# Wider matmuls for the head-norm sums and the spatial bias in a hybrid decoder kernel

## The chip, the cores and the metric

The program runs on all 8 NeuronCores of one Trainium2 chip. Each core works on one prompt sequence of 2048 tokens and on 16 of the 128 sample sequences (8 tokens each); the cores exchange nothing. The metric is the device time of the slowest core, in microseconds (us).

Some executions fall in a second, slower state, in which the cores of a die (cores 0 to 3 or 4 to 7) are granted a lower TensorE clock. Ratios below use fast runs only; a median is over all runs of a kernel, slow ones too, so a median of a kernel with several slow runs says little. Even in fast runs a pair of cores can be a little slow (clock 0.97 in place of 0.98), and the slowest of eight is a noisy number. For effects of a few us I therefore also use the **core mean**: the mean span of the cores of a run, averaged over the runs of a kernel, without cores whose granted clock is more than 0.007 below the median clock of that kernel. The "±" beside a core mean is twice the standard error over executions.

## The reference, cut to what matters

Two layers; each mixes three branches and then runs a feed-forward block. The change touches two places:

```python
# branch A: the output of the gated linear attention, per head of 256 channels
o = rms_norm(o, gla_norm) * jax.nn.silu(g_out)
# branch C: spatial gating within chunks of 128 positions, 4 head groups
w = w_s * tril
mixed = jnp.einsum('gts,ncsgd->nctgd', w, vg) + b_s.T[None, None, :, :, None]
return u * mixed
```

## The kernel before: the parts that matter

All matmuls but the transposes go through one helper. It waits for the operands, issues a list of matmuls and lets the last one signal. In the tuples the fourth and fifth entries are `start` and `stop` of an accumulation. All of these matmuls show up in the profile under the helper's line, L219.

```python
def pe_group(mms, reads, writes, late=None):
    acquire(PE, reads, writes)
    for i, m in enumerate(mms):
        ...
        inst = nc.tensor.matmul(m[0], m[1], m[2], start=m[3], stop=m[4], **kw)
    t = PE.tok(inst)            # the last matmul signals
    release(t, ...)
```

A token tile has 128 tokens; a core has 17 tiles per layer. Activations lie channels on partitions, tokens along the columns. The head norm needs, for each head and token, the sum of 256 squares: two halves of 128 channels. A matrix of ones sums over partitions.

```python
def o_norm(l, ov, ob, gt, gB, Hout, HB):
    ps = psum()
    for h in range(4):
        for a in range(2):
            pe_group([(ps.t[:, h * 128:(h + 1) * 128], ones_bf.t[:, :], sqg.t[:, 2 * h + a, :], a == 0, a == 1)],
                     [sqg, ones_bf], [ps])
    act(rsg.t[:, :], ps.t[:, :], AF.Ln, [ps], [rsg], bias=EPS, scale=1.0 / 256)
    act(rsg.t[:, :], rsg.t[:, :], AF.Exp, [rsg], [rsg], scale=-0.5)
    yield 1
    ...                          # VectorE: tmp4 = o * norm weight * rsg, in two instructions
    yield 1
    tt(Hout, tmp4.t[:, :, :], gt, ALU.mult, [tmp4, gB], [HB])

def gla_scan(l, b):              # runs in the background, a step at each `yield`
    ...
    act(sqg..., OV, AF.Square, OB_, [sqg])
    yield 1
    ...                          # state update: 4 matmuls, VectorE and ScalarE
    yield 1
    yield from o_norm(l, OV, OB_, ...)
```

The generator `gla_scan` is stepped between the projection matmuls of the next tiles, so the head norm of one tile overlaps with projections of another. PE issues in program order: if a background step is not ready when its turn comes, PE waits.

The spatial gating of a tile makes four 128-column maps, and adds the bias `b[t]` by a matmul of ones with a tile whose first row holds the bias:

```python
def sgate(b, j):
    ps = psum()
    mms = []
    for g in range(4):
        osl = ps.t[:, g * 128:(g + 1) * 128]
        wv = wsS.t[:, g, :] if smp else wsT.t[:, g, :]
        bv = bsS.t[:, g, :, :].rearrange("o i t -> o (i t)") if smp else bsp.t[:, g, :]
        mms += [(osl, vtk.t[:, j, g * 128:(g + 1) * 128], wv, True, False, True),
                (osl, ones_bf.t[:, :], bv, False, True, True)]
    pe_group(mms, ...)
    tt(OBC..., ps..., uT..., ALU.mult, [ps, uT], [OBC])
```

## Time and profile before

| | before |
|---|---|
| time, median of 4 runs (lowest, one slow run as highest) | 2558.51 us (2556.18, 2946.33) |
| spans of the cores in the profiled run | 2550.2 to 2554.7 us |
| granted clock of the cores | 0.982 to 0.985 |
| matmuls on the slowest core | 13828 |

The profile's page gives the busy time of each engine with its share of the span and its number of instructions. This is its line for core 3, the slowest, with the head of the chain of waits (the chain of work that ended last, followed back from the end, by engine):

```profile
PE 2395.8 (94%) x13828; PEld 1257.5 (49%) x13828; DVE 1254.9 (49%) x2112; ACT 967.7 (38%) x1803; POOL 77.2 (3%) x98
...
PE 82%; DVE 5%; ACT 5%; DMA 4%; issue 3%; DVEq 0%; ACTq 0%; POOL 0%; SPq 0%; POOLq 0%
```

PE is the matmul side of TensorE, PEld its weight loads, DVE is VectorE and ACT is ScalarE. PE looks like the limit. Windows of the same core, one row per stretch of time (start and end, length, then busy us of each engine, the granted clock, the DMA share and the DMA rate), show that this is an average of two kinds of stages:

```profile
120.00:465.00 345.00, 299.46 (x2085) 168.47 (x2083) 214.42 (x412) 205.71 (x355) 8.51 (x10) 0.96 0.44 103
465.00:1357.00 892.00, 883.24 (x4792) 454.11 (x4790) 398.50 (x624) 259.55 (x504) 29.91 (x37) 1.00 0.40 78
1357.00:1701.00 344.00, 310.43 (x2121) 172.92 (x2120) 216.91 (x416) 205.34 (x360) 8.53 (x10) 0.97 0.44 103
1701.00:2554.00 853.00, 832.71 (x4377) 422.91 (x4375) 376.45 (x566) 223.96 (x439) 18.98 (x22) 0.99 0.33 71
```

The second and fourth rows (merge, output and feed-forward of the two layers) have PE busy 99% and 98% of the time. The first and third rows are the mixers, and only these hold the two groups that change. There PE is busy 87% and 90%, and VectorE and ScalarE some 60%.

Now the two groups. The timeline of PE merges neighbours of one kind into a row: start, length, and at the end the number of instructions. First a head-norm group, then a spatial group (the sample tile):

```profile
121.71 0.61 PE L219 MATMUL ps<-sqg,ones_bf 128*128 128x128 bf16 x8
122.16 1.46 PE L219 MATMUL ps<-hn,wring 128*128 128x384 bf16 x8
...
362.80 0.22 PE L219 MATMUL ps<-wsS,vtk 128*128 128x128 bf16 x1
362.86 0.22 PE L219 MATMUL ps<-bsS,ones_bf 128*128 128x128 bf16 x1
362.91 0.22 PE L219 MATMUL ps<-wsS,vtk 128*128 128x128 bf16 x1
...
363.19 0.22 PE L219 MATMUL ps<-bsS,ones_bf 128*128 128x128 bf16 x1
363.25 1.46 PE L219 MATMUL ps<-hn,wring 128*128 128x384 bf16 x8
```

Each 128-column matmul lasts 0.22 us, but the next one starts 0.05 to 0.06 us later: the lengths overlap. What a matmul costs is the step from its start to the next start. The eight matmuls of the head norm take from 121.71 to 122.16, and the eight of the spatial group from 362.80 to 363.25, 0.45 us each. Taken over all groups, from the start times in the trace, the median group of either kind takes 447 ns, eight times 56; a 512-column matmul takes 216 ns (median of 6703).

### The profile page before, as it was taken

What the parts mean: (1) busy time and instruction counts of PE and PEld (TensorE: products, weight loads), DVE (VectorE), ACT (ScalarE), POOL (GpSimd) and SP (SyncE); (2) the same over time, 40 slices, a digit from 0 to 9 for tenths busy, and PEclk for the clock granted to TensorE, in tenths of its full rate; (3) what the DMA queues carried; (4) which work ended last, traced back from release to release, by engine and by line L of the source; (5) the groups of instructions that cost most, each with busy time, mean ns of one, the idle gap of its engine ahead of it and who ended that gap; (6) DMA issues with size and microseconds to landing.
All of it is one profiled execution on the core that took longest, in us unless ns stands there. A gap on an engine that the chain in (4) does not pass through costs nothing.

```text
span 2554.7 us, 40653 instructions; the slowest of 8 cores (2550.2 to 2554.7 us)
## 1 busy us (share of the span) xinstructions
PE 2395.8 (94%) x13828; PEld 1257.5 (49%) x13828; DVE 1254.9 (49%) x2112; ACT 967.7 (38%) x1803; POOL 77.2 (3%) x98
## 2 busy tenths in 40 slices
PE   3889979999999999999999898899999999999997
PEld 1544544555544545445555545455464454545453
DVE  2566655444445444444556666544443554444455
ACT  4866654322225311112555666532222441111133
POOL 1000000000000000000000000000000000000000
PEclk9999989999999999999999999999999999999999
DMA  9534732727236222315272347262450932222112
GB/s 178 107 100 125 138 80 75 149 63 128 83 64 168 42 34 34 43 24 68 76 146 84 96 119 133 75 133 79 77 116 32 214 59 33 34 34 33 17 50 91
DMA packets 176673, 219.27 MB, mean 86 GB/s; under 512 B 12978, under 2 KB 160826, under 8 KB 173368
## 3 DMA queue, kind: packets, MB, share of 16 engines
q0 software_dynamic: 81024, 78.07, 22.8%
q1 hardware_dynamic: 95448, 138.62, 17.2%
q8 instruction: 115, 1.88, 0.3%
q14 instruction: 86, 0.70, 0.1%
HBM read 240.12 MB, written 55.05 MB: 116 GB/s over the span
## 4 chain that ended last, share of the span: by engine, by line
PE 82%; DVE 5%; ACT 5%; DMA 4%; issue 3%; DVEq 0%; ACTq 0%; POOL 0%; SPq 0%; POOLq 0%
PE ps L219 81%; PE ps L228 1%; ACT L190 1%; DMA OB_d<-OBC_118 1%; DVE tmp_100 L196 1%; DMA wn<-nvec 1%; DMA wsp<-w_spT 1%; DMA wgk_bf<-w_gk 1%; ACT rsg L190 1%; DMA wring<-w_in 1%; DVE pt_115 L193 0%; DVE pt_116 L193 0%; DVE lv L661 0%; DVE go_85 L193 0%; ACT OBC_118 L190 0%
## 5 line engine op out<-in xcount | busy, mean ns | idle before, releaser
L219 PE MATMUL ps<-hn,wring 128*128 128x384 bf16 (+1 forms) x6400 | 1257.5, 350 | 37.1 <-ACT xfS L190 11.0
L219 PEld LDWEIGHTS ps<-hn,wring 128*128 128x128 bf16 x6400 | 623.1, 98 | 581.7 <-issue 56.4
L190 ACT ACTIVATE rl_139<-ps 128x384 f32<-128x384 f32 (+1 forms) x160 | 85.4, 534 | 487.5 <-PE ps L219 432.8
L219 PE MATMUL ps<-wring,a_1_138 128*128 128x512 bf16 x1088 | 238.6, 379 | 0.0
L219 PE MATMUL ps<-wring,a_0_137 128*128 128x512 bf16 x1088 | 238.3, 379 | 0.0
L219 PE MATMUL ps<-wring,hn 128*128 128x512 bf16 x848 | 205.1, 391 | 24.0 <-DMA wring<-w_in 17.1
L219 PEld LDWEIGHTS ps<-wring,a_0_137 128*128 128x128 bf16 x1088 | 106.3, 98 | 127.0
L219 PEld LDWEIGHTS ps<-wring,a_1_138 128*128 128x128 bf16 x1088 | 106.3, 98 | 126.3
L190 ACT ACTIVATE sg_133<-ps 128x384 f32<-128x384 f32 (+1 forms) x120 | 64.1, 534 | 237.3 <-PE ps L219 155.2
L190 ACT ACTIVATE sg_134<-ps 128x384 f32<-128x384 f32 (+1 forms) x120 | 64.1, 534 | 221.5 <-PE ps L219 156.5
L219 PEld LDWEIGHTS ps<-wring,hn 128*128 128x128 bf16 x848 | 81.8, 100 | 121.1 <-issue 40.7
L190 ACT ACTIVATE rl_140<-ps 128x384 f32<-128x384 f32 (+1 forms) x160 | 85.5, 534 | 138.8 <-PE ps L219 65.2
L193 DVE TENSOR_TENSOR tmp_135<-sg_133,ps 128x384 f32<-128x384 f32 (+1 forms) x80 | 48.6, 608 | 82.3 <-ACT sg_133 L190 44.4
L193 DVE TENSOR_TENSOR a_0_137<-rl_139 128x384 bf16<-128x384 f32 (+1 forms) x80 | 49.0, 612 | 80.8 <-ACT rl_139 L190 80.5
L193 DVE TENSOR_TENSOR a_1_138<-rl_139 128x384 bf16<-128x384 f32 (+1 forms) x80 | 48.9, 612 | 75.2 <-ACT rl_139 L190 74.6
L196 DVE SCALAR_TENSOR_TENSOR tmp_100<-ps,vec_t,rsg 128x512 f32<-128x512 f32 x68 | 51.0, 750 | 68.0 <-ACT rsg L190 60.6
L193 DVE TENSOR_TENSOR tmp_136<-sg_134,ps 128x384 f32<-128x384 f32 (+1 forms) x80 | 48.7, 609 | 68.8 <-ACT sg_134 L190 35.1
L193 DVE TENSOR_TENSOR a_1_138<-rl_140 128x384 bf16<-128x384 f32 (+1 forms) x80 | 48.9, 612 | 64.6 <-ACT rl_140 L190 63.9
L193 DVE TENSOR_TENSOR a_0_137<-rl_140 128x384 bf16<-128x384 f32 (+1 forms) x80 | 48.9, 612 | 63.9 <-ACT rl_140 L190 63.4
L219 PE MATMUL ps<-OBs_127,wring 128*128 128x384 bf16 (+1 forms) x320 | 72.5, 350 | 7.2 <-DVE acc_129 L193 7.2
L190 ACT ACT_TABLE_LOAD x55 | 70.6, 1283 | 21.7 <-PE ps L219 14.2
L190 ACT ACTIVATE hn<-ps 128x1024 bf16<-128x1024 bf16 x68 | 69.3, 1019 | 23.1 <-PE ps L228 22.9
(450 smaller groups left out, 2631.3 us busy)
## 6 DMA issues: line engine op xcount, KB each, us to landing
wring<-w_ff POOLq DMA_DIRECT2D x32, 1024.0 KB, 15.5
wring<-w_in POOLq DMA_DIRECT2D x30, 1024.0 KB, 15.5
H4s_125<-H_d SPq DMA_DIRECT2D x6, 768.0 KB, 15.0
OBs_127<-OB_d SPq DMA_DIRECT2D x6, 768.0 KB, 11.9
H4s_126<-H_d SPq DMA_DIRECT2D x6, 768.0 KB, 14.0
OBs_128<-OB_d SPq DMA_DIRECT2D x6, 768.0 KB, 5.6
Sf_90<-sgla SPq DMA_DIRECT2D x16, 256.0 KB, 3.0
Sf_91<-sgla SPq DMA_DIRECT2D x16, 256.0 KB, 2.9
```

What stands on the lines that cost most here:

```text
L190: return op(ACT, lambda: nc.scalar.activation(out=out, in_=in_, func=func, **kw), reads, writes)
L193: return op(DVE, lambda: nc.vector.tensor_tensor(out=out, in0=in0, in1=in1, op=alu), reads, writes)
L196: return op(DVE, lambda: nc.vector.scalar_tensor_tensor(out=out, in0=in0, scalar=scalar, in1=in1, op0=op0, op1=op1), reads, writes)
L219: inst = nc.tensor.matmul(m[0], m[1], m[2], start=m[3], stop=m[4], **kw)
L228: inst = nc.tensor.transpose(o, i, ident_ap)
```

## The change

The intent: fewer and wider instructions for the same arithmetic. The squares of one half of all four heads are read as one 512-column operand (four runs of 128 columns with gaps between), so two matmuls make the sums of four heads; the bias is one 512-column matmul that starts the accumulation, and the four maps are added onto it.

```diff
     def o_norm(l, ov, ob, gt, gB, Hout, HB):
         ps = psum()
-        for h in range(4):
-            for a in range(2):
-                pe_group([(ps.t[:, h * 128:(h + 1) * 128], ones_bf.t[:, :], sqg.t[:, 2 * h + a, :], a == 0, a == 1)], [sqg, ones_bf], [ps])
+        sv = sqg.t[:, :, :].rearrange("p (h a) t -> p a h t", a=2)
+        pe_group([(ps.t[:, :].rearrange("p (h t) -> p h t", h=4), ones_bf.t[:, :], sv[:, a], a == 0, a == 1) for a in range(2)], [sqg, ones_bf], [ps])
@@ sgate
-        mms = []
+        bv = bsS.t[:, :, :, :].rearrange("o g i t -> o (g i t)") if smp else bsp.t[:, :, :].rearrange("o g t -> o (g t)")
+        mms = [(ps.t[:, :], ones_bf.t[:, :], bv, True, False, True)]
         for g in range(4):
-            osl = ps.t[:, g * 128:(g + 1) * 128]
             wv = wsS.t[:, g, :] if smp else wsT.t[:, g, :]
-            bv = bsS.t[:, g, :, :].rearrange("o i t -> o (i t)") if smp else bsp.t[:, g, :]
-            mms += [(osl, vtk.t[:, j, g * 128:(g + 1) * 128], wv, True, False, True), (osl, ones_bf.t[:, :], bv, False, True, True)]
+            mms.append((ps.t[:, g * 128:(g + 1) * 128], vtk.t[:, j, g * 128:(g + 1) * 128], wv, False, True, True))
```

## The prediction

> **What bounds the kernel.** The page gives PE 2395.8 us busy of a 2554.7 us span (94%), VectorE 49%, ScalarE 38%; the chain of waits puts 82% on PE, nearly all of it on the one matmul helper line. The clock is granted at 0.98 on every core. In the two long stages (465 to 1357 us and 1701 to 2554 us, by windows) PE is busy 99% and 98%; the change touches neither, only the two mixer stages (120 to 465 us and 1357 to 1701 us), where PE is busy 87% and 90%.
>
> **What the change does.** Per token tile there are one head-norm group and one spatial group, 17 tiles by 2 layers, 34 of each.
> - Head norm: 8 matmuls of 128 columns become 2 of 512. 1024 columns streamed, before and after.
> - Spatial: 4 maps and 4 biases of 128 columns become 1 bias of 512 and 4 maps of 128. Again 1024 columns.
> - So 306 of 13828 matmuls go, and as many weight loads (272 to 68 on the squares, 136 to 34 on the biases); multiply work is the same. The instruction order on VectorE, ScalarE, GpSimd and SyncE is unchanged. Each head-norm group signals once, not eight times.
>
> **Cost, from the trace.** The groups by form list 128-column matmuls at about 220 ns and 512-column ones at 379 ns. Those are latencies, not costs. What counts is start to next start. From the timeline's start times: 128 columns 56 ns, 512 columns 216 ns (median of 6703). An eight-matmul group of either kind takes 447 ns from its first start to the start of the next matmul where nothing waits: eight times 56. The 98 ns weight loads, the alternating weights of the spatial group and the eight signals cost nothing visible: they hide behind the stream.
>
> The Trainium skill, "TensorE: Matmul & The Clock Gate" (section "Back-to-back issue gap"), states N/2.4 + 2.5 ns for a warm gap, 56 and 216 ns; this trace agrees to the nanosecond. Its other figure, about 81 ns for 128 columns in a stream with weight loads, does not fit this trace, and the trace decides.
>
> After: head norm 2 x 216 = 432 ns (15 ns less per group), spatial 216 + 4 x 56 = 440 ns (7 ns less). Estimate: 34 x 15 + 34 x 7 = 0.75 us, 0.03%. Mostly on the critical path, perhaps 0.5 us arrives.
>
> **Predicted time.** 2559 us, from 2559.97, range 2551 to 2567. The spread of the fast runs before (2556.2, 2556.8, 2560.0) is larger than the gain. Faster by over 2%: 0.01; within 2%: 0.98; slower: 0.01.
>
> **What would show it.** 13522 matmuls and loads. Weight-load busy falls by some 20 us (272 loads on the squares take 17.5 us of busy time, 128 of the prompt biases 12.7 us) without the span following. Head-norm matmuls start 216 ns apart, the bias matmul is followed by its first map 216 ns later, maps stay at 56 ns. VectorE and ScalarE busy times are unchanged.
>
> **What would make it wrong.** The head-norm moving operand is now four runs of 128 columns with gaps; no operand in the trace before has that shape at 512 columns. Were it to stream at half rate, 68 x 216 = 14.7 us more (0.6%), still within 2%. If weight loads do cost time I can't see (through the clock granted, say), the gain could reach some 20 us, 0.8%.

## More of the kernel before

The chain of waits of the first part of a mixer (120 to 360 us, core 3) says more:

```profile
by line: PE ps L219 51.2%; issue 10.7%; DMA wsp<-w_spT 7.6%; ACT L190 3.2%; DVE tmp_100 L196 3.1%; ACT rsg L190 1.9%; ACT lv L190 1.3%; DVE Sf_90 L196 1.3%; DVE Sf_93 L196 1.1%; DVE Sf_91 L196 1.1%; ACT eb_73 L190 1.0%; DVE U_96 L196 1.0%; 
```

In this part only half of the chain is PE. The end of the mixer is another stage. The same view of 403 to 465 us:

```profile
by line: PE ps L219 98.4%; ACT OBC_118 L190 1.1%; ACT xf L190 0.6%; issue 0.2%
```

So the mixer is not one stage but two. In the first layer all 17 head-norm groups start before 400 us, and 11 of the 17 spatial groups start after 403 us.

The experiments ran on three chips; the core means of the kernel before on them are 2550.4, 2550.2 and 2549.6 us, so they can be compared.

## The result, and the profile after

| | before | after |
|---|---|---|
| time, median of 4 runs | 2558.51 us | 2556.14 us |
| lowest to highest | 2556.18 to 2946.33 us | 2554.8 to 2559.03 us |
| ratio of fast runs, 95% interval | | 0.9995 (0.9976 to 1.0015) |
| matmuls | 13828 | 13522 |
| weight-load busy time, core 3 | 1257.5 us | 1244.9 us |

A ratio here is the mean time of one kernel's fast runs over the mean of the other's fast runs of the same rounds, so it is not quite the ratio of the medians. The result is correct.

The profile after, on core 3, the core shown before (it is not the slowest now): busy times, and the head of the chain of waits.

```profile
PE 2397.9 (94%) x13522; PEld 1244.9 (49%) x13522; DVE 1255.5 (49%) x2112; ACT 967.2 (38%) x1803; POOL 77.2 (3%) x98
...
PE 82%; DVE 6%; ACT 5%; DMA 4%; issue 3%; DVEq 0%; ACTq 0%; POOL 0%; SPq 0%; POOLq 0%
```

The same four windows, columns as before:

```profile
120.00:465.00 345.00, 299.49 (x1932) 161.60 (x1930) 214.50 (x412) 205.01 (x355) 8.51 (x10) 0.96 0.44 102
465.00:1357.00 892.00, 883.37 (x4774) 453.81 (x4772) 395.92 (x618) 256.76 (x496) 29.91 (x37) 0.99 0.40 78
1357.00:1701.00 344.00, 309.12 (x1979) 166.27 (x1978) 218.94 (x421) 208.98 (x368) 7.69 (x10) 0.98 0.43 102
1701.00:2554.00 853.00, 834.05 (x4390) 423.77 (x4388) 377.65 (x567) 223.44 (x440) 19.81 (x23) 0.99 0.33 72
```

The first mixer has 153 matmuls less in its window, weight-load busy time is down from 168.47 to 161.60 us, and PE busy time is what it was (299.46, 299.49). Fewer instructions did not show as less busy time. The timeline of the same two groups, core 3:

```profile
122.36 0.59 PE L219 MATMUL ps<-sqg,ones_bf 128*128 128x512 bf16 x2
122.79 0.81 PE L219 MATMUL ps<-hn,wring 128*128 128x384 bf16 x4
...
363.80 0.38 PE L219 MATMUL ps<-bsS,ones_bf 128*128 128x512 bf16 x1
364.02 0.39 PE L219 MATMUL ps<-wsS,vtk 128*128 128x128 bf16 x4
364.24 0.33 PE L219 MATMUL ps<-hn,wring 128*128 128x384 bf16 x1
```

The head norm takes from 122.36 to 122.79 and the spatial group from 363.80 to 364.24. In ns, the medians over all groups are 432 (2 x 216) and 439. The operand with gaps streams at the rate of a plain one (216 ns). So the two groups are 15 and 8 ns shorter, and 34 of each make 0.8 us.

### The profile page after: what moved, and what is told of

Read it like the earlier page. It is cut to its first block, busy times and chain, and to the rows that moved or that the text cites. A ratio compares the mean times of both kernels' runs of the same rounds, so it can differ in the third digit from the quotient of the medians.

```text
span 2558.0 us, 40041 instructions; the slowest of 8 cores (2540.3 to 2558.0 us)
## 1 busy us (share of the span) xinstructions
PE 2398.9 (94%) x13522; PEld 1244.7 (49%) x13522; DVE 1255.8 (49%) x2112; ACT 968.1 (38%) x1803; POOL 77.4 (3%) x98
## 4 chain that ended last, share of the span: by engine, by line
PE 82%; DVE 5%; ACT 5%; DMA 4%; issue 3%; DVEq 0%; ACTq 0%; POOL 0%; SPq 0%; POOLq 0%
PE ps L219 81%; PE ps L228 1%; DMA OB_d<-OBC_118 1%; DMA wn<-nvec 1%; ACT L190 1%; DMA wsp<-w_spT 1%; DVE tmp_100 L196 1%; DMA wgk_bf<-w_gk 1%; DMA wring<-w_in 1%; ACT rsg L190 0%; DVE pt_115 L193 0%; ACT OBC_118 L190 0%; DVE U_96 L196 0%; DVE lv L661 0%; DVE pt_116 L193 0%
## 6 DMA issues: line engine op xcount, KB each, us to landing
H4s_126<-H_d SPq DMA_DIRECT2D x6, 768.0 KB, 14.5
```

## The experiments

Saving 0.8 us is far below what a run resolves, so the first four runs repeat the groups until the difference can be seen. The rest ask what PE time in the mixers is worth, because the prediction said that it is mostly on the critical path.

### Head-norm sums repeated, 128 columns

```diff
-        for h in range(4):
+        for h in [0, 1, 2, 3] * 21:
             for a in range(2):
                 pe_group([(ps.t[:, h * 128:(h + 1) * 128], ones_bf..., sqg.t[:, 2 * h + a, :], a == 0, a == 1)], ...)
```

> The kernel before with each head-norm group of eight 128-column matmuls issued 21 times, every matmul pair-step with its own signal as before; result unchanged. Theory (only the columns and about 2.5 ns per matmul cost anything): 56 ns from start to start throughout, so 34 x 20 x 447 ns = 304 us more, less what covers waits that stand now (up to some 40 us): 2820 to 2865 us. Rival 1 (weight loads or the eight signals cost time once there are many in a row): a steady cadence above 60 ns, up to about 80 ns, which would be 435 us or more.

Measured: 2802.85 us, ratio to before 1.0965 (1.0929 to 1.1001), core mean 2796.9 ± 0.6. Timeline, core 3:

```profile
119.80 9.54 PE L219 MATMUL ps<-sqg,ones_bf 128*128 128x128 bf16 x168
129.18 1.46 PE L219 MATMUL ps<-hn,wring 128*128 128x384 bf16 x8
```

168 matmuls, each with its own weight load and its own signal, take 9.38 us: 55.8 ns each. The cadence is that of the theory, and rival 1 is out. The total missed my range at the low end: 304 us more of PE work made the core mean 247 us longer, so 57 us were covered, not 40. Waits that stood before can cover them, and so can the clock, as the granted clock rose from some 0.984 to 0.991; the two were not told apart.

### Head-norm sums repeated, 512 columns

```diff
-        pe_group([(..., sv[:, a], a == 0, a == 1) for a in range(2)], ...)
+        pe_group([(..., sv[:, a], a == 0, a == 1) for a in [0, 1] * 21], ...)
```

> The changed kernel with each head-norm group of two 512-column matmuls (four runs of 128 columns with gaps) issued 21 times; result unchanged. Theory: 216 ns from start to start, 34 x 20 x 432 ns = 294 us more, less covered waits: 2810 to 2855 us, and 10 us (21 x 34 x 15 ns = 10.7 us) under the 128-column run of the same chip. Rival 1 (loads or signals cost): under it by 100 us and more. Rival 2 (the gapped read costs something that eats the gain): a cadence above 216 ns and no gain over the 128-column run.

Measured: 2796.82 us, ratio 1.0949 (1.0901 to 1.0997), core mean 2789.6 ± 1.0. Timeline, core 3:

```profile
120.59 9.23 PE L219 MATMUL ps<-sqg,ones_bf 128*128 128x512 bf16 x42
129.66 1.46 PE L219 MATMUL ps<-hn,wring 128*128 128x384 bf16 x8
```

42 matmuls in 9.07 us, 216 ns each. In ns a repeated group is 9065 against 9380, 315 less, which over 34 groups is 10.7 us of PE time. The core mean is 7.2 us lower, the median 6.0. The total missed its range (2810 to 2855) at the low end, as in the run before. Neither a cost of loads or signals (100 us expected) nor of the gaps is there.

### Spatial groups repeated, before and after

```diff
-        pe_group(mms, ...)
+        pe_group(mms * 21, ...)
```

This is one run with the old list of matmuls and one with the new list.

> The kernel before with each spatial group (map, bias, map, bias ... of 128 columns, weights changing at every matmul, one signal per 21) issued 21 times; result unchanged. Theory: 56 ns cadence, 34 x 20 x 447 ns = 304 us more less covered waits, the same as the repeated head-norm run, although there the weights stay the same and each matmul signals: 2820 to 2865 us. Rival 1 (changing weights or signals cost): the two runs differ by tens of us.

Measured: 2828.53 us, ratio 1.1052 (1.1024 to 1.1080), core mean 2822.8 ± 1.7. A repeated group takes 9380 ns, to the nanosecond what the head norm's takes, although here the weights change at every matmul and only the last one signals. (In this trace 189 matmul records of the slowest core are missing; where one is missing a step looks 216 ns longer.) The core mean is 26 us higher than that of the head-norm run. Most spatial groups start where the chain of waits is 98.4% PE and leaves no waits to cover extra work, and no head-norm group does; that would explain it, but no run tested it. So "the same as the repeated head-norm run" held for the cadence and not for the time.

> The changed kernel with each spatial group (one 512-column bias, four 128-column maps) issued 21 times; result unchanged. Theory: 216 + 4 x 56 = 440 ns a group, 34 x 20 x 440 ns = 299 us more less covered waits; 5 us (21 x 34 x 7.5 ns = 5.4 us) under the 128-column spatial run. Rival (merging the bias saves loads that matter): under it by 20 us or more.

Measured: 2821.92 us, ratio 1.1028 (1.1001 to 1.1054), core mean 2816.5 ± 1.1. A repeated group takes 9223 ns, 157 less, over 34 groups 5.3 us; the core mean is 6.3 ± 2.0 us lower. The rival (20 us or more) is out.

### Where would merging pay? Narrower matmuls

```diff
+        for w in (64, 32, 16):
+            pe_group([(ps.t[:, h * 128 + c:h * 128 + c + w], ones_bf.t[:, :], sqg.t[:, 2 * h + a, c:c + w], a == 0, a == 1)
+                      for h in range(4) for c in range(0, 128, w) for a in range(2)], [sqg, ones_bf], [ps])
         pe_group([... the two 512-column matmuls ...])
```

> The changed kernel with the head-norm sums first made three more times from narrower matmuls: 16 of 64 columns, 32 of 32, 64 of 16, each with its weight load; result unchanged. It shows where merging would pay. Theory N/2.4 + 2.5 ns with nothing else: 29, 16 and 9 ns from start to start. Rival (a fixed floor per matmul and weight load): the step stops falling at some value, at least the 25 ns that the 8-column matmuls of this kernel show, so the three groups take 0.46 or more, 0.8 or more and 1.6 us or more, against 0.43 us for 512 columns.

Measured in one run, correct: the medians of the step are 29 ns at 64 columns, 25 ns at 32 and 25 ns at 16. There is a floor of 25 ns, weight load included. The time of 1024 columns is then 0.43 us at 512 columns, 0.45 at 128, 0.46 at 64, 0.80 at 32 and 1.60 at 16. "TensorEngine Tiling (Array Packing)" of the Trainium skill, section "Instruction Overhead", says that each matmul has an overhead of about 60 cycles, so that one column costs as much as 60; at the 2.4 GHz that the skill's "TensorE: Matmul & The Clock Gate" gives in section "What's actually happening", 60 cycles are 25 ns (an estimate), and this run agrees. Merging pays below some 54 columns (an estimate: there 2.5 ns and the columns at 2.4 GHz reach 25 ns), and hardly above. The extra matmuls were 97 us of PE time (34 x 2.86 us), and the core mean rose by 49 us.

### What PE time is worth here: one 512-column matmul out of every group

```diff
-        pe_group([(..., sv[:, a], a == 0, a == 1) for a in range(2)], ...)
+        pe_group([(..., sv[:, a], True, True) for a in range(1)], ...)
@@ sgate
-        mms = [(ps.t[:, :], ones_bf.t[:, :], bv, True, False, True)]
+        mms = []
-            mms.append((..., wv, False, True, True))
+            mms.append((..., wv, g == 0, True, True))
```

> The changed kernel with one 512-column matmul taken out of each of the 68 groups: the head-norm sums cover only the first half of each head, and the spatial bias is left out. WRONG RESULT ON PURPOSE. It measures what PE time in these two stages is worth: 68 x 216 ns = 14.7 us of PE time less. Theory (PE is the limit there): 8 to 15 us less than the changed kernel, 0.3 to 0.6%; group lengths 216 and 224 ns. Rival (these matmuls stand in time in which PE would wait anyway): no difference within 0.2%.

The result is wrong. Measured: 2554.04 us, ratio to before 1.0003 (0.9953 to 1.0052; one of the fast runs had two cores at a clock of 0.963), core mean 2545.0 ± 1.1 against 2549.4 of the changed kernel. The groups took 216 and 223 ns, as expected. Of 14.7 us of PE time 4.4 ± 1.4 us arrived, 30% (20 to 40%). The expectation of 8 to 15 us is missed, and 4.4 us is 0.17%, within the 0.2% that the rival allowed, though not nothing. The waits of PE in the first mixer (core 3; in total, how many, the longest) show part of where the rest went. First the changed kernel:

```profile
PE ps L219 <- DVE kq_78 L193: 4.7, 4, 2.6
...
PE ps L219 <- ACT lv L190: 3.4, 5, 0.9
PE ps L219 <- ACT xf L190: 3.3, 5, 1.6
...
PE ps L219 <- DVE kq_79 L193: 1.8, 2, 1.2
```

Then the kernel with the matmuls taken out (here the two `kq` buffers are one row):

```profile
PE ps L219 <- DVE kq L193: 6.7, 6, 2.6
PE ps L219 <- ACT lv L190: 4.1, 7, 0.9
...
PE ps L219 <- ACT xf L190: 3.8, 6, 1.6
...
PE ps L219 <- ACT vtk L190: 2.0, 2, 1.1
```

No single wait took the time. `kq` waits are the same (6.5 against 6.7); waits for the tiles `lv`, `xf` and `vtk`, which ScalarE writes, became more or longer, by 0.5 to 2 us each; all waits of PE in this mixer together grew from 44.5 to 49.3 us. PE gets to its next operand sooner, and the operand is not there yet. Over both mixers (each from its first `wglr` matmul to the first matmul of the merge), mean of the eight cores of the profiled runs, the matmuls themselves (summed as columns / 2.4 GHz + 2.5 ns, at least 25 ns each, which fits the measured steps) took 14.5 us less, and the mixers became 2.9 us shorter (830.8 to 827.9 us): 1.9 us in the two parts before the first spatial matmul, 1.0 us in the two parts after it.

A second loss shows in the later part of the mixer, from its first spatial matmul to the merge. Two cores of the same profiled run, windows 360 to 400, 400 to 408 and 408 to 465 us; first core 1, whose part took 100.5 us:

```profile
360.00:400.00 40.00, 32.86 (x202) 17.88 (x201) 26.81 (x53) 26.63 (x43) 0.00 (x0) 0.91 0.08 26
400.00:408.00 8.00, 6.41 (x43) 3.65 (x42) 3.62 (x7) 5.19 (x12) 0.00 (x0) 1.00 0.51 197
408.00:465.00 57.00, 57.00 (x305) 27.72 (x303) 34.31 (x56) 25.27 (x44) 2.64 (x3) 1.00 0.50 105
```

Then core 3, whose part took 103.8 us:

```profile
360.00:400.00 40.00, 31.86 (x204) 17.54 (x202) 26.83 (x54) 26.75 (x44) 0.00 (x0) 0.96 0.08 27
400.00:408.00 8.00, 5.73 (x24) 2.55 (x25) 3.80 (x8) 5.18 (x12) 0.00 (x0) 0.66 0.51 197
408.00:465.00 57.00, 57.00 (x301) 27.56 (x299) 33.41 (x55) 24.44 (x42) 2.37 (x3) 0.99 0.42 94
```

Look at the clock (third figure from the right) and the number of matmuls (first bracket) in the middle rows. At 400 us core 3 was granted 0.66 of the clock just as its dense stretch began, and started 24 matmuls where core 1 started 43. The Trainium skill, "TensorE: Matmul & The Clock Gate", section "What's actually happening", describes a gate that halves the clock after an idle window of about 3.4 us. This run agrees in the lengths: the clock records of the trace show stretches at half clock, most of them 3.4 or 6.8 us long, five to nine per core in each mixer. But PE need not have been idle: in the 3.4 us before such a stretch the matmuls (summed as above) filled up to 45% of the time, 22% in the median. Whether such a stretch hits waiting or work differs from core to core. In the changed kernel the first layer's later part took 102.6 to 104.2 us on all eight cores; with the matmuls out, four cores took 100.5 us, the others 102.3 to 103.9. In the second layer one core took 100.5 us, the others 102.4 to 104.0. The lengths go with the clock on every core. Of the 16 later parts of this run (8 cores, 2 layers), the five without a half-clock stretch after the first 37 us took 100.5 us; the two with one of about 3.4 us took 102.3 and 102.4; the nine with one of about 6.8 us took 103.7 to 104.0. In the changed kernel the ten without took 102.5 to 102.6 us (one more, with a single stretch at another place, 103.3) and the five with one of 3.4 us 104.1 to 104.2. So where the clock leaves it alone, the later part gains 2.1 us per layer, most of the 2.4 us that the eleven bias matmuls after 403 us take (216 ns each). There PE is the limit, and half-clock stretches took most of the gain back in this profiled run. That the clock makes this difference is read from the records, not tested by a run.

### Can VectorE take work from PE? Halves added before the sum

```diff
             act(sqg..., OV, AF.Square, OB_, [sqg])
             yield 1
+            tt(sqg.t[:, 0:8:2, :], sqg.t[:, 0:8:2, :], sqg.t[:, 1:8:2, :], ALU.add, [sqg], [sqg])
 ...
-        pe_group([(..., sv[:, a], a == 0, a == 1) for a in range(2)], ...)
+        pe_group([(..., sv[:, a], True, True) for a in range(1)], ...)
```

The same addition follows the square of the sample tile.

> The changed kernel with the two halves of the squares of a head added on VectorE (one in-place addition of 128x512 bf16, 34 of them), so that one 512-column matmul makes the head-norm sums; result right within rounding. PE streams 34 x 216 ns = 7.3 us less. Theory: 3 to 7 us less than the changed kernel if the addition (about 0.3 to 0.6 us each, 10 to 20 us of VectorE in all) hides, as VectorE is 62% busy in these stages. Rival: the addition delays the chain square, sum, Ln, or the evacuations queued behind it, and the gain is gone: the same or slower, with new PE waits for VectorE on the squares.

Measured, correct: 2567.7 us, ratio 1.0022 (0.9994 to 1.0049), core mean 2553.5 ± 1.3, which is 4.1 ± 1.5 us more than the changed kernel. The rival is right. In the waits of PE (core 3) a new row stands:

```profile
PE ps L219 <- DVE sqg L193: 15.0, 5, 4.3
```

The addition takes 419 ns, 14.2 us over 34; it sits between the square and the sum, and PE waits for it.

### Less work on ScalarE: half of the squares

```diff
-            act(sqg.t[:, :, :]..., OV, AF.Square, OB_, [sqg])
+            act(sqg.t[:, :, :].rearrange("p (h a) t -> p h a t", a=2)[:, :, 0, :], o_view(OV)[:, :, 0, :], AF.Square, OB_, [sqg])
 ...
-        pe_group([(..., sv[:, a], a == 0, a == 1) for a in range(2)], ...)
+        pe_group([(..., sv[:, 0], a == 0, a == 1) for a in range(2)], ...)
```

> The changed kernel with the prompt tiles' squares taken of one half of each head only (ScalarE 128x512 in place of 128x1024, about 0.5 us less for each of 32 tiles, 15 us of ScalarE in all), that half used twice in the sums; PE issues the same matmuls. WRONG RESULT ON PURPOSE. Theory after the run that took matmuls away (the scan part of the mixer waits for the chain through ScalarE and VectorE, not for PE): the scan parts get shorter by 2 to 10 us in all. Rival (PE time is what counts there, and the missing gain of that run is noise): no change, within 1 us of the mean over the undisturbed cores.

The arithmetic is wrong (the error stayed within the tolerance of the comparison; it is no version to keep). Measured: 2554.83 us, ratio 0.9982 (0.9967 to 0.9998), core mean 2545.2 ± 1.7, so 4.2 ± 1.9 us less than the changed kernel. The square fell from 1020 to 594 ns, 13.6 us over 32 tiles, so again about 30% arrived. Within the noise ScalarE time is worth as much here as PE time.

### Less work on VectorE: half of the last multiplication

```diff
-        tt(Hout, tmp4.t[:, :, :], gt, ALU.mult, [tmp4, gB], [HB])
+        n = KT if gB is goS else KT // 2
+        tt(Hout[:, 0:n], tmp4.t[:, 0:n, :], gt[:, 0:n], ALU.mult, [tmp4, gB], [HB])
```

> The changed kernel with the last multiplication of the prompt head norm done on half of its columns (VectorE 128x512 in place of 128x1024, about 0.6 us less for each of 32 tiles, 19 us of VectorE in all); PE and ScalarE do the same. WRONG RESULT ON PURPOSE. Theory: VectorE is in the chain too, so the scan parts get shorter by 2 to 10 us in all; more than by less ScalarE work if VectorE holds the chain, less if ScalarE does. Rival (PE): no change.

Its output is wrong, which doesn't matter for the time. Measured: 2563.67 us, ratio 0.9989 (0.9927 to 1.0051; three of its eight runs were slow and count in the median alone, and one fast run had a pair of slower cores), core mean 2541.5 ± 1.5, so 7.9 ± 1.7 us less. The multiplication fell from 1216 to 682 ns, 17.1 us over 32 tiles, and 46% arrived. Of the three engines VectorE has the highest share, though 46 ± 10% against 30 ± 10% is only just clear of the noise.

### The changed kernel again, and a version from these runs

The first is the changed kernel unaltered, to have it in the same rounds as the second. The second keeps the intermediate of the head norm in bf16:

```diff
-    tmp4 = sba("tmp4", [128, KT, 128], F32, RM + 4 * KB)
+    tmp4 = sba("tmp4", [128, KT, 128], BF16, RM + 4 * KB)
```

> The changed kernel once more, unaltered, in the same rounds and on the same chip as the next one and as a direct companion to the kernel before: 2555 to 2558 us, mean of the undisturbed cores 2549 to 2551 us. If the change is worth 0.75 us of PE time, of which the other runs say about a third arrives, no difference from before can be resolved (under 1 us in the core means).

Measured: 2565.71 us median over all runs (three of six fast runs had a pair of cores at 0.97), 2553.2 to 2555.5 in the other three; ratio 0.9997 (0.9955 to 1.0038). Core mean 2549.4 ± 1.2, against 2549.5 ± 0.6 in its first four runs and 2550.1 ± 0.5 of the 44 runs of the kernel before beside the experiments (one has no undisturbed core). The difference is some 0.7 us with an uncertainty of about 1 us. The trace shows what a slower pair is: cores 0 and 1 were granted 0.81 of the clock for one stretch of 161 us (from 363 us on), while cores 2 and 3 of the same die had 0.97 over the same time.

> The changed kernel with the intermediate of the head norm (normed heads before the gate) kept in bf16 instead of f32, so that the last multiplication reads and writes bf16 only; result right within rounding. If that multiplication falls from 1.22 us to about 0.6 us (the addition of 128x512 bf16 operands of an earlier run gives the rate), VectorE has 20 us less work, as in the run that halved it, and the core means fall by 5 to 8 us (0.2 to 0.3%) to about 2542 to 2545 us. Rival: the gain of that run came from its wrong data or from a lucky state, and nothing falls.

Measured, correct: 2560.68 us median, ratio 0.9981 (0.9940 to 1.0023), so on the slowest core nothing is resolved: four of its six runs had a pair of cores at a clock of 0.975. The two others took 2543.74 and 2544.72 us, below the lowest run of before in the same rounds (2554.25). The core mean is 2539.6 ± 1.2, 9.8 ± 1.5 us or 0.4% under the changed kernel, more than the 5 to 8 us expected. The groups of VectorE by form (count, busy us, mean ns) show why. The changed kernel, core 3:

```profile
L193 DVE TENSOR_TENSOR go_85<-tmp_100,go_85 128x1024 bf16<-128x1024 f32 x18 | 21.9, 1216 | 0.1
L193 DVE TENSOR_TENSOR go_86<-tmp_100,go_86 128x1024 bf16<-128x1024 f32 x14 | 17.0, 1216 | 0.8 <-DVE tmp_100 L196 0.5
```

With the intermediate in bf16, core 3:

```profile
L193 DVE TENSOR_TENSOR go<-tmp,go 128x1024 bf16<-128x1024 bf16 x32 | 21.8, 682 | 0.9 <-DVE tmp L196 0.5
```

The Trainium skill, "VectorE: DVE Perf Modes", section "The perf-mode tier table", gives `tensor_tensor` twice the rate when its operands are bf16 in SBUF; here 1216 became 682 ns, 1.8 times. That is 17.1 us over 32 tiles, of which 57% arrived. One changed type on VectorE was worth more than 306 fewer matmuls on the busiest engine.

## Why the prediction was right, and where it was not

- **Time: right.** 2559 us within 2551 to 2567 was predicted, 2556.14 us was measured. This hit alone says little: the range is 16 us wide, and a gain of nothing or of ten times the forecast would have fallen in it. What the runs confirm is the cost of a matmul, below.
- **"What counts is start to next start": right, and shown.** 56 and 216 ns stand after the change and in trains of 168 and 42 matmuls. The group lengths of 432 and 440 ns were measured as 432 and 439 ns.
- **Weight loads, alternating weights and eight signals "cost nothing visible": right, and shown** by the repeated head-norm and spatial groups, which differ in both of the last two and take the same 9380 ns. The prediction chose the skill's 56 ns over its 81 ns because the trace already showed 56; the trains confirm the choice.
- **The gapped operand as a risk: it did not come.** It streams at 216 ns.
- **"Mostly on the critical path": not confirmed, and the runs speak against it.** This is the weak step. It rested on the page's 82% of the chain and on 87 to 90% of busy time in the mixers. The chain of waits by part would have said before any run that it holds for the end of the mixer (98.4% PE) and not for the part before it (51% PE from 120 to 360 us), where the head-norm groups stand. Taking 14.7 us of PE time away brought 4.4 us. At that rate the change is worth about 0.25 us of its 0.8, not the 0.5 predicted; the measured 0.7 ± 1 us fits both, so for the change itself this is open.
- **Weight-load busy "falls by some 20 us": mis-sized.** It fell by 12.6 us (core 3). The loads overlap: in the spatial groups the loads of maps and biases took 13.4 and 13.5 us counted apart but 17.7 us together, and 13.3 us after the change, so 4.4 us went where I had counted some 10. The head-norm loads fell by 11.7 us, and all others rose by 2.5. That the span would not follow was right.

What limits the mixers as a whole is then no single engine, though from about 403 us on it is PE. A microsecond taken from PE, ScalarE or VectorE brought 0.3, 0.3 and about 0.5 us, and one added to PE cost 0.5 (97 us added), 0.8 (some 300 us added to the head norm) or 0.9 (some 300 us added to the spatial groups). Each cut of head-norm work also shortened the chain of square, sum, logarithm and multiplication that a tile goes through, so the time of an engine and the length of this chain are not told apart; work taken from ScalarE or VectorE outside this chain was not tried. Which dependence of the background chain holds each tile was not settled.

## What to carry to other kernels

Cost a matmul by the step from its start to the next one's, not by its recorded length or by its weight load: in the trains here that step was 216 ns at 512 columns, 56 at 128, 29 at 64 and 25 at 32 and 16. So merging matmuls at the same number of columns pays much only when they are narrower than some 54 columns (the estimate above). A high busy share of an engine over a whole kernel says little about a stage, and a stage can have parts with different limits: follow the chain of waits in the stage, or take some of the work away (even at the price of a wrong result) and see what arrives. Where work is spread over coupled engines, look for the cheapest microsecond on any of them.

## What the Trainium skill lacked or had wrong

- "TensorE: Matmul & The Clock Gate", section "Back-to-back issue gap": the sustained figures for streams of weight load and matmul (about 81 ns at 128 columns, 131 ns at 512) do not hold here: 55.8 and 216 ns in trains of 168 and 42 pairs. The figures that it calls isolated (56 and 216) are the right ones for the stream.
- The same page, section "The cost: per-tile semaphore tail", gives 26 ns for each further signal of concurrent tiles, and does not say that in a train of full-size matmuls no such cost adds up: 168 matmuls that all signal take 9380 ns, as 168 with one signal do. (Here a signal comes every 56 ns, so the two need not conflict.)
- The same page, section "Seeing it yourself", expects 13/16 of the clock whenever three cores of a die run dense matmuls. Here all eight cores run them, with PE busy 98 to 99% in the long stages, and most executions are granted 0.98. The level itself does occur: two of the traces have one stretch of about 160 us at 0.81 of the clock, but on two cores of a die and not on all four. What brings it on is not shown.
- "TensorE: Matmul & The Clock Gate" gives no cost for a moving operand with gaps: four runs of 128 columns stream at 216 ns, as one run of 512.
